# A hybrid residual block on one core: four seven-product pairs in the second feed-forward, a weight sum made by accumulating transfers, and four engines' issue order written out as a table

## The chip, the cores and the metric

The kernel runs on one core of a Trainium2 chip. The metric is the device time of one launch in microseconds (us). Engines: TensorE (PE in the rows), VectorE (DVE), ScalarE (ACT), GpSimd (POOL) and SyncE (SP, which issues most loads); transfers run on 16 DMA engines. Each engine takes its instructions in the order in which they were written to its queue and waits where an operand isn't ready.

## The reference

One layer of an encoder block on x of 256 tokens x 1024 channels, in float32:

```python
h = rmsnorm(x, ffn1_pre_g)
x = x + 0.5 * rmsnorm(swiglu(h, ffn1_w_in, ffn1_w_down), ffn1_post_g)
h = rmsnorm(x, mix_pre_g)              # gated recurrence, forgetting attention, merge
...
x = x + rmsnorm(y @ w_out, mix_post_g)
x = x + rmsnorm(mem_cross_attention(...), mem_post_g)
h = rmsnorm(x, ffn2_pre_g)
x = x + 0.5 * rmsnorm(swiglu(h, ffn2_w_in, ffn2_w_down), ffn2_post_g)

def swiglu(h, w_in, w_down):           # w_in 1024 x 5632, w_down 2816 x 1024
    gate, up = split(h @ w_in, 2)
    return (silu(gate) * up) @ w_down
```

The change concerns the second `swiglu`, and the order of everything.

## The kernel before

Every product is made of three: a float32 weight tile `raw` of 128x1024 is loaded (512 KB), ScalarE rounds it to `hi` and VectorE subtracts, `lo = raw - hi` (`load_split`, L151 to L155; `split`, L173 and L174, for tiles that are computed). PE then multiplies activation-hi by weight-hi, activation-hi by weight-lo and activation-lo by weight-hi, each a 128x512 matmul (`MM`, L100). There are 8 `hi` and 8 `lo` buffers, 4 `raw` ones and 4 of a tag "extra", whose tiles are called `sraw`.

A feed-forward (`ffn`, from L427) cuts its 2816 hidden columns into 11 chunks of 256 (512 columns of w_in, gate and up). A chunk is done directly (`act_tok`, `act_col`, `act_first`: 2 halves of the tokens x 8 blocks of channels x 3 = 48 matmuls, 4 weight tiles), or two chunks together as a pair (`act_pair`). A pair does the 2x2 block product (token halves by channel halves, and the weight's channel halves by the two chunks) with seven block products in place of eight, by sums of the blocks: 7 x 12 = 84 matmuls for two chunks. Its weight operands are, in order: `sums` (first loaded as one block, `of_x(0)`), then `sums + both`, then that plus block (1,1), block (1,1) itself, `both` plus block (1,1), block (1,0), and last the sum plus block (1,0). Each is two tiles, split to hi and lo (`splits`). The block sums are made either by VectorE (`add`, L596) or, for the pairs in the list FETCHED, by POOL with an accumulating load into the tile (`more`, L569, `both[j]` += block (1,1)). VectorE takes the four quarter results together (`c01` L645, `c11` L651, `c00` L661); `act_evac` does silu on ScalarE (L450) and the product with the up half on VectorE (L453, L455) to `at`; `flush` transposes `at` on PE (L445) to `tr` and splits it to `act`; `down` multiplies `act` by w_down into four accumulators. The downs of older chunks stand between a pair's products.

In the second feed-forward chunks 0, 1, 2, 5 and 8 are direct, and (3,4), (6,7) and (9,10) are pairs. Its tail is `post` (L416 to L421), which adds to `xs` and stores.

The order of each engine's queue is made by a scheduler from the order of the program, with hooks where it was corrected by hand: `tc.high_priority()`, `tc.issue_after(ins)`, and `after(i)`, which puts work behind the i-th matmul. At the start the weights come with the first layer's input in tiles `head`; ScalarE casts them (L828), makes `hlT` (L372) and `xf` (L832).

Of the kernel before, what the change touches and what calls it, by code (L numbers as in the profile page):

```python
# [18 lines left out]
P = 128  # L19
# [16 lines left out]
TOKS = {"f1_in": (3, 8), "f2_in": (2, 5, 8)}  # L36

PAIRS = {"f1_in": (4, 6, 9), "f2_in": (3, 6, 9)}
# [17 lines left out]
FETCHED = {"f1_in": (4, 6, 9), "f2_in": (3, 6, 9)}  # L56
# [11 lines left out]


# [16 lines left out]
def block_kernel(ctx: ExitStack, tc: tile.TileContext, wts, head_in, gf_in, x_in, mem_in, memT_in, cols, rows, fbias, masks, out):  # L86
    nc = tc.nc
    V, S, G, PE = nc.vector, nc.scalar, nc.gpsimd, nc.tensor

    cp = ctx.enter_context(tc.tile_pool(name="consts", bufs=1))  # L90
# [10 lines left out]

    @contextmanager
    def after(i):

        with tc.high_priority(), tc.issue_after(log[min(i, len(log) - 1)]):
            yield
# [37 lines left out]
    def load_split(src, n=512, behind=None, parts=None):  # L144

        raw = wp.tile([P, D], F32, tag="raw", name=nm("raw"), bufs=4)
        hi, lo = parts or parts_of()
        r, h, l = raw, hi, lo
        if n < 512:
            r, h, l = (p.rearrange("p (k n) -> p k n", k=2)[:, :, :n] for p in (raw, hi, lo))  # L150
        loads.append(nc.sync.dma_start(r, src).ins)  # L151
        with tc.issue_after(behind[0]) if behind else nullcontext():
            casts.append(S.copy(h, r).ins)  # L153
        with tc.issue_after(behind[1]) if behind else nullcontext():
            los.append(V.tensor_tensor(out=l, in0=r, in1=h.bitcast(F32), op=ALU.subtract).ins)  # L155
        return hi, lo
# [138 lines left out]
    def table(ins):  # L295

        with tc.issue_after(ins):
            S.activation(warm, ones[:, 0:1], AF.Abs_reciprocal_sqrt)
# [128 lines left out]
    def ffn(w_in, w_dn, X, r2, n_tok, i_row, first_half, second_half=None):  # L427
# [8 lines left out]
        def flush(n):  # L436

            if late:
                c = late.pop(0)
                tr = trp()  # L440
                trv = tr.rearrange("p (j t) -> p j t", j=2)
                with after(n):
                    for h in range(2):
                        for j in range(2):
                            PE.transpose(trv[:, j, h * P : (h + 1) * P], ats[c, h][:, j * P : (j + 1) * P], ident)  # L445
                    split(acts[c][:, 0], acts[c][:, 1], trv)
# [87 lines left out]
        def pair_inputs():  # L534
            for k in range(2):
              with tc.issue_after(evs[-1][1]):
                V.tensor_tensor(out=xf[k][:, :, P:], in0=xf[k][:, :, P:], in1=bc(row[:, :P], [P, 4, P], 1), op=ALU.mult)
# [33 lines left out]
        def act_pair(c, between):  # L571
# [55 lines left out]
            with tc.issue_after(last_silu[0]) if c - 2 in pairs else nullcontext():  # L627
                u = splits(sums)
# [5 lines left out]
            u = splits(sums)  # L634
            if "e" not in sx:
# [7 lines left out]
            with tc.high_priority():  # L643
                t = half_tile("c01")
                V.tensor_tensor(out=t, in0=b4, in1=v, op=ALU.subtract)  # L645
                act_evac(t, c, 0)
            product(b1, of("ad"), splits(both), False)
            S.copy(w, b1)
            with tc.high_priority():
                t = half_tile("c11")  # L650
                V.tensor_tensor(out=t, in0=p5, in1=w, op=ALU.subtract)  # L651
                act_evac(t, c, 1, r2[0], q)
# [5 lines left out]
            add(sums, raw)  # L658
            with tc.high_priority():
                t = half_tile("c00")  # L660
                V.tensor_tensor(out=t, in0=p1, in1=b0, op=ALU.add)  # L661
                act_evac(t, c + 1, 0)
# [7 lines left out]
            with tc.high_priority():  # L670
                silu = act_evac(b1, c + 1, 1, r2[0], q)
# [8 lines left out]
        def pair_loads(c):  # L680
            if c in pairs and c not in sums_of_pair:
                with tc.issue_after(loads[-1]):
                    sums_of_pair[c] = sum_load(c, 0, ((0, 0), (0, 1))), sum_load(c, 1, ((0, 1), (1, 1)))
# [17 lines left out]
        if callable(r2):  # L701
# [4 lines left out]
            for c in range(2):  # L706
                acts[c] = m4([P, 2, 2, T], F32R, "act")
                for h in range(2):
                    with tc.issue_after(casts[-1]):
                        silu = act_evac(outs[c][h], c, h)  # L710
# [3 lines left out]
        for c in range(n_tok, NFF):  # L714
# [42 lines left out]
            if c <= 6 <= last:  # L757
                grow = load_row(i_row)
                if first_half:
                    with tc.issue_after(loads[-1]):  # L760
                        nc.sync.dma_start(masks_s, masks)
# [58 lines left out]
    for kb in range(KB):  # L820
# [3 lines left out]
        for c in range(2):  # L824
            hi, lo = (p[:, kb % 2 * 512 : kb % 2 * 512 + 512] for p in cache[_AT["f1_in"] + 4 * c + kb // 2])
            w = heads[kb][:, HX : HX + 512] if c == 0 else raw1[kb // 2][:, kb % 2 * 512 : kb % 2 * 512 + 512]
            with tc.issue_after(lo_last):
                S.copy(hi, w)  # L828
# [5 lines left out]
    def norm_1():  # L834
        with tc.issue_after(loads[X_AT]):
            for h in range(2):
                nc.sync.dma_start(xs[:, h], x_in[:, h])
        with tc.issue_after(loads[-1]):
            nc.sync.dma_start(cols_s, cols)
            nc.sync.dma_start(fb_s, fbias)  # L840
# [7 lines left out]
    def half(X, r, h, g, *ms, into=None, act=True):  # L848

        for i, m in enumerate(ms):  # L850
            with after(m):
                to_T(X, x_blocks(h), h, g, (i,) if len(ms) == 2 else (0, 1), mm if X is X3 and h else trp)
# [30 lines left out]
    with tc.issue_after(iv_last):  # L883
        S.activation(le, le, AF.Exp)
# [220 lines left out]
    def forget(m):  # L1105
        pf = trp()
        with after(m):
            for h in range(2):
                PE.transpose(pf[0:8, h * P : (h + 1) * P], zf[h], ident)
        V.tensor_scalar(out=fz, in0=pf[0:8, :T], scalar1=fb_s, scalar2=None, op0=ALU.add)  # L1110
        V.scalar_tensor_tensor(out=fa, in0=fz, scalar=-1.0, in1=fz, op0=ALU.mult, op1=ALU.max)
        with tc.issue_after(sig_last):
            logs.append(S.activation(fa, fa, AF.Exp, scale=-1.0).ins)
# [37 lines left out]
    with after(r0):  # L1151
        for r in recs:
            r.grow(0)
    for si, ms in enumerate(SETS):
        with after(r0 + R_AT[si]):
            banks = [acc()]
            banks.append(acc() if ms[-1] in (1, 128) else banks[0])
            for j, m in enumerate(ms):
                for r in recs:
                    r.products(m, banks[r.g if m == 128 else j], j == 1)  # L1160
            with tc.issue_after(gf_last[1, 1]) if si == 1 else tc.issue_after(lo_at["k_b", 1]) if ms[-1] == 64 else nullcontext():
                for r in recs:
                    if ms[-1] < 128:
                        r.grow(ms[-1])
            with tc.issue_after(logs[1]) if ms[-1] == 32 else nullcontext():
                for m in ms:
                    for r in recs:
                        r.keep(m, LEVELS.index(m) if m < 64 else None)
        if si == FG:
            with tc.high_priority(), tc.issue_after(recs[1].grown):  # L1170
                forget_sums()
        if si < 2:
            with tc.high_priority(), tc.issue_after(gf_last[R_GROW[si]]):
                for r in recs:
                    r.grow(SETS[si + 1][0])
# [4 lines left out]
    for g in range(2):  # L1180
        kp = [wp.tile([P, D], F32R, tag="extra", name=nm("kp"), bufs=4).rearrange("p (i t) -> p i t", i=4) for _ in range(2)]
        qp = m4([P, 2, 4, P], F32R, n="qp")
        with tc.high_priority():
            for j in range(2):
                i2 = slice(2 * j, 2 * j + 2)
                with tc.issue_after(recs[1].last) if (g, j) == (0, 1) else nullcontext():
                    split(kp[0][:, i2], kp[1][:, i2], kb_[g][:, i2])
            for j in range(2):
                i2 = slice(2 * j, 2 * j + 2)
                split(qp[:, 0, i2], qp[:, 1, i2], qb_[g][:, i2, P:])  # L1190
# [67 lines left out]
    def fox_pT(g, m):  # L1258
        pT0 = m4([P, 4, T], n="pT0")
        pT1 = wp.tile([P, D], F32, tag="extra", name=nm("pT1"), bufs=4)[:, :512].rearrange("p (i s) -> p i s", i=4)  # L1260
        for h, b in ((0, 0), (1, 0), (1, 1)):
            tr = trp()
            with after(m + 5 * b):
                for i in range(4):
                    PE.transpose(tr[:, i * P : (i + 1) * P], ps_[g, h][:, i, b * P : (b + 1) * P], ident)
                trv = tr.rearrange("p (i s) -> p i s", i=4)
                if b == 0:
# [545 lines left out]
```

## Time and profile before

| | us |
|---|---|
| median of 3 runs | 767.94 (767.77 to 768.22) |
| the profiled execution | 767.82 |
| its span in the profile | 765.6 |
| from the second feed-forward's begin to the end of the span | 575 to 765.6 |
| the stretch from its chunk 5 on to the last lo | 629.4 to 742.4 |

The span goes from the first to the last instruction that the profile shows; 2.2 us of the execution lie outside of it. The clock granted to PE was 0.998 of full. "PE" in a row is the matmul, "PEld" its weight load. A row `L155 DVE TENSOR_TENSOR lo<-raw,hi ... x38 | 45.7, 1220 | 3.2 <-ACT hi L153 3.1` means: 38 instructions of line 155 on VectorE, 45.7 us busy, 1220 ns each, and 3.2 us idle ahead of them, of which 3.1 waiting for line 153 on ScalarE. Two instructions of an engine can overlap by some 0.1 us, so the time from one start to the next is what a row of them costs.

### The profile page before, as it was taken

The page shows a single profiled execution, that of the slowest core. Times are in us where ns is not written, and L with a number is a line of the kernel's source. Part 1 is how long each engine was busy: PE and PEld are TensorE (multiplying, and loading weights), DVE is VectorE, ACT ScalarE, POOL GpSimd, SP SyncE. Part 2 cuts the span into 40 slices and gives each one's busy share as a digit, 9 for nine tenths or more (in the row PEclk, how much of TensorE's full clock was granted, in tenths as well). Part 3 has the DMA queues.
Part 4 walks back from the last instruction along what each step waited for, and adds up shares of the span by engine and source line. Part 5 has one row for each costly group of instructions (what it writes and reads, how often), then busy time and mean ns, then how long its engine had stood idle before and what let it go on. Part 6 is the DMA issues. An engine that isn't in the chain of part 4 may idle for free.

```text
span 765.6 us, 11756 instructions
## 1 busy us (share of the span) xinstructions
PE 756.7 (99%) x4302; PEld 642.8 (84%) x4302; DVE 664.4 (87%) x982; ACT 521.2 (68%) x841; POOL 33.0 (4%) x56
## 2 busy tenths in 40 slices
PE   9999999999999999999999999999999999999996
PEld 8888888888888998898888888888887888888885
DVE  6799998988678898888689899999979899997973
ACT  8667576688774659667666755875968566675762
POOL 0000000000000100200001000001000100000000
PEclk9999999999999999999999999999999999999999
DMA  9778777674745545835668955586386837868641
GB/s 350 235 259 245 214 239 275 182 252 167 233 158 149 185 137 183 284 128 182 189 220 245 267 183 186 175 286 131 114 291 191 257 108 257 236 222 269 176 131 55
DMA packets 47146, 157.88 MB, mean 206 GB/s; under 512 B 5385, under 2 KB 9105, under 8 KB 47089
## 3 DMA queue, kind: packets, MB, share of 16 engines
q1 hardware_dynamic: 43168, 144.83, 55.5%
q0 software_dynamic: 3488, 11.94, 8.7%
q8 instruction: 33, 0.54, 0.3%
q10 hardware_dynamic: 432, 0.37, 0.2%
q14 instruction: 25, 0.20, 0.1%
HBM read 156.06 MB, written 1.06 MB: 205 GB/s over the span
## 4 chain that ended last, share of the span: by engine, by line
PE 85%; DVE 8%; ACT 2%; DMA 2%; issue 1%; DVEq 0%; ACTq 0%
PE mm L100 45%; PE acc L100 33%; PE tr L100 5%; DVE lo L155 2%; DMA raw<-in_wts_dram 2%; PE tr L445 1%; DVE lo L174 1%; ACT hi L153 1%; PE tr L385 1%; DVE xs L421 1%; DVE sraw L1393 1%; DMA head<-in_head_dram 0%; DVE post L416 0%; DVE sx L174 0%; DVE qm L1578 0%
## 5 line engine op out<-in xcount | busy, mean ns | idle before, releaser
L155 DVE TENSOR_TENSOR lo<-raw,hi 128x1024 fp32r<-128x1024 f32 (+1 forms) x188 | 222.3, 1199 | 29.5 <-ACT hi L153 26.2
L153 ACT CAST hi<-raw 128x1024 fp32r<-128x1024 f32 (+1 forms) x188 | 190.9, 1033 | 50.3 <-DMA raw<-in_wts_dram 29.7
L100 PE MATMUL mm<-hi,hlT 128*128 128x512 f32 (+1 forms) x632 | 191.6, 382 | 0.0
L100 PEld LDWEIGHTS mm<-hi,hlT 128*128 128x128 f32 x632 | 116.7, 188 | 20.2
L100 PE MATMUL mm<-lo,hlT 128*128 128x512 f32 (+1 forms) x316 | 119.1, 381 | 0.0
L100 PE MATMUL acc<-hi,act 128*128 128x512 f32 x352 | 113.6, 390 | 0.0
L173 ACT CAST hi<-sraw 128x1024 fp32r<-128x1024 f32 x80 | 83.3, 1052 | 33.9 <-DVE sraw L596 15.6
L174 DVE TENSOR_TENSOR lo<-sraw,hi 128x1024 fp32r<-128x1024 f32 x80 | 96.1, 1221 | 3.8 <-ACT hi L173 3.4
L100 PE MATMUL mm<-hi,sx 128*128 128x512 f32 x280 | 90.8, 391 | 0.0
L100 PEld LDWEIGHTS acc<-hi,act 128*128 128x128 f32 x352 | 66.2, 188 | 13.4
L100 PE MATMUL acc<-lo,act 128*128 128x512 f32 x176 | 69.5, 395 | 0.0
L100 PEld LDWEIGHTS mm<-lo,hlT 128*128 128x128 f32 x316 | 59.3, 188 | 10.0
L100 PEld LDWEIGHTS mm<-hi,sx 128*128 128x128 f32 x280 | 52.5, 188 | 10.9
L100 PE MATMUL acc<-hlT,hi 128*128 128x512 f32 x240 | 60.7, 394 | 0.0
L100 PE MATMUL mm<-lo,sx 128*128 128x512 f32 x140 | 54.9, 392 | 0.0
L100 PEld LDWEIGHTS acc<-hlT,hi 128*128 128x128 f32 x240 | 43.1, 189 | 7.7 <-DVE hlT L373 0.2
L174 DVE TENSOR_TENSOR lo<-raw,hi 128x1024 fp32r<-128x1024 f32 x32 | 38.6, 1221 | 2.1 <-ACT hi L173 2.0
L173 ACT CAST hi<-raw 128x1024 fp32r<-128x1024 f32 x32 | 33.1, 1053 | 8.5 <-issue 3.1
L100 PEld LDWEIGHTS acc<-lo,act 128*128 128x128 f32 x176 | 33.1, 188 | 6.4
L100 PE MATMUL acc<-lo,hT 128*128 128x512 f32 x96 | 37.8, 393 | 0.0
L100 PE MATMUL acc<-hi,hT 128*128 128x512 f32 x96 | 37.7, 392 | 0.1
L100 PE MATMUL acc<-hi,lT 128*128 128x512 f32 x96 | 37.3, 391 | 0.0
(329 smaller groups left out, 1232.4 us busy)
## 6 DMA issues: line engine op xcount, KB each, us to landing
raw<-in_wts_dram SPq DMA_DIRECT2D x215, 512.0 KB, 4.6
sraw<-in_wts_dram SPq DMA_DIRECT2D x32, 512.0 KB, 6.6
sraw<-in_wts_dram POOLq DMA_DIRECT2D x20, 512.0 KB, 5.9
raw<-in_gf_dram SPq DMA_DIRECT2D x12, 344.0 KB, 3.7
head<-in_head_dram SPq DMA_DIRECT2D x7, 392.0 KB, 6.4
grow<-in_rows_dram SPq DMA_DIRECT2D x4, 512.0 KB, 7.6
xs<-in_x_dram SPq DMA_DIRECT2D x2, 512.0 KB, 7.6
cb<-cd POOLq DMA_DIRECT2D x2, 512.0 KB, 4.9
```

The lines of the kernel that those rows point to most:

```text
L100: log.append(PE.matmul(*args, **kw).ins)
L153: casts.append(S.copy(h, r).ins)
L155: los.append(V.tensor_tensor(out=l, in0=r, in1=h.bitcast(F32), op=ALU.subtract).ins)
L173: a = S.copy(hi, src)
L174: b = V.tensor_tensor(out=lo, in0=src, in1=hi.bitcast(F32), op=ALU.subtract)
L385: PE.transpose(blocks[-1][1], src(kb), ident)
L421: summed = V.scalar_tensor_tensor(out=xh, in0=ts[a // 512][:, a % 512 : (b - 1) % 512 + 1], scalar=r, in1=xh, op0=ALU.mult, op1=ALU.add)
L445: PE.transpose(trv[:, j, h * P : (h + 1) * P], ats[c, h][:, j * P : (j + 1) * P], ident)
L1393: V.tensor_tensor(out=x, in0=x, in1=y, op=ALU.add)
```

## The change

1. In the second feed-forward TOKS becomes (2,) and PAIRS (3, 5, 7, 9): chunks 5 and 8 are no longer direct, and 3 to 10 are four pairs in a row. FETCHED names all four.
2. A new list FETCHED_LAST (those four pairs): the last product's weight sum is made by two accumulating loads of block (1,0) on POOL's queue, issued behind the third split, in place of two additions on VectorE. Block (1,0) is still loaded on its own for the product before.
3. All hooks are taken out. `issue()`, called at the end, reads a table ISSUE with the complete order of PE's, VectorE's, ScalarE's and SP's instructions, as runs "first+count" of the program's own numbering, and chains each instruction to the one before it. POOL's order is not in the table.

```diff
-TOKS = {"f1_in": (3, 8), "f2_in": (2, 5, 8)}
-
-PAIRS = {"f1_in": (4, 6, 9), "f2_in": (3, 6, 9)}
+TOKS = {"f1_in": (3, 8), "f2_in": (2,)}
+
+PAIRS = {"f1_in": (4, 6, 9), "f2_in": (3, 5, 7, 9)}
...
-FETCHED = {"f1_in": (4, 6, 9), "f2_in": (3, 6, 9)}
+FETCHED = {"f1_in": (4, 6, 9), "f2_in": (3, 5, 7, 9)}
+FETCHED_LAST = {"f1_in": (), "f2_in": (3, 5, 7, 9)}
...
+ISSUE = {
+    "PE": (
+        "0+124 154+2 124+6 156 130+10 157+2 140+6 159+2 146+8 161+25 190+14 186 204+20 187+3 224+28 286+3 252+34 290+8 289 298+73 386 371+14 387+2 385 390+6 "
...
+    def issue():
+        traced = [i for i in nc.cur_bb.bb.instructions if i.opcode != "TilePoolBoundary"]
+        for name, runs in ISSUE.items():
+            own = [i for i in traced if i.engine == getattr(mybir.EngineType, name)]
+            order = []
+            for run in runs.split():
+                first, _, n = run.partition("+")
+                order += own[int(first) : int(first) + int(n or 1)]
+            assert len(order) == len(own), (name, len(order), len(own))
+            for before, ins in zip(order, order[1:]):
+                tc.add_manual_dep(ins, before.name, mybir.DependencyInfo(mybir.DependencyClass.NoSync, mybir.DependencyReason.DATA))
...
-                with after(n):
-                    for h in range(2):
-                        for j in range(2):
-                            PE.transpose(trv[:, j, h * P : (h + 1) * P], ats[c, h][:, j * P : (j + 1) * P], ident)
-                    split(acts[c][:, 0], acts[c][:, 1], trv)
+                for h in range(2):
+                    for j in range(2):
+                        PE.transpose(trv[:, j, h * P : (h + 1) * P], ats[c, h][:, j * P : (j + 1) * P], ident)
+                split(acts[c][:, 0], acts[c][:, 1], trv)
...
-            with tc.issue_after(last_silu[0]) if c - 2 in pairs else nullcontext():
-                u = splits(sums)
+            u = splits(sums)
...
             raw = raws(1, 1)
             add(sums, raw)
             u = splits(sums)
+            if c in FETCHED_LAST[w_in]:
+                for j in range(2):
+                    more(sums[j], c, 1, 0, j, ALU.add)
...
-            add(sums, raw)
-            with tc.high_priority():
-                t = half_tile("c00")
-                V.tensor_tensor(out=t, in0=p1, in1=b0, op=ALU.add)
-                act_evac(t, c + 1, 0)
+            if c not in FETCHED_LAST[w_in]:
+                add(sums, raw)
+            t = half_tile("c00")
+            V.tensor_tensor(out=t, in0=p1, in1=b0, op=ALU.add)
+            act_evac(t, c + 1, 0)
```

The instructions by engine, before and after: PE 3966 and 3954 (12 matmuls of 128x512 fewer; 210 transposes in both, in 48 runs before and 110 after, of which 64 are of one), VectorE 984 and 991, ScalarE 782 and 793 (one of them a table load more), POOL 61 and 71, SP 292 in both, in another order.

What the table and the pairs do to the queues is seen at four places. In the rows a name ends in two numbers, of the name and of the buffer's tile; line numbers of the changed kernel are higher (L248 is the `split` subtraction, L667 `add`, L640 the accumulating load, L182 `MM`, L517 `flush`, L894 the head's cast).

VectorE, third weight operand of the second pair in the chain. Before, in pair (6,7):

```order
L453 TENSOR_TENSOR at_1454_6941<-mm_1452_6914,sg_1453_6939 128x256
L596 TENSOR_TENSOR sraw_1455_6943<-sraw_1455_6943,raw_1480_7046 128x1024
L596 TENSOR_TENSOR sraw_1456_6945<-sraw_1456_6945,raw_1481_7047 128x1024
L174 TENSOR_TENSOR lo_1483_7053<-sraw_1455_6943,hi_1482_7052 128x1024
L174 TENSOR_TENSOR lo_1485_7057<-sraw_1456_6945,hi_1484_7056 128x1024
```

Now, in pair (5,6):

```order
L667 TENSOR_TENSOR sraw_1435_6853<-sraw_1435_6853,raw_1460_6956 128x1024
L248 TENSOR_TENSOR act_1363_6536<-tr_1432_6842,act_1363_6536 128x512
L248 TENSOR_TENSOR lo_1459_6928<-sraw_1436_6855,hi_1458_6927 128x1024
L248 TENSOR_TENSOR lo_1463_6963<-sraw_1435_6853,hi_1462_6962 128x1024
L667 TENSOR_TENSOR sraw_1436_6855<-sraw_1436_6855,raw_1461_6957 128x1024
L248 TENSOR_TENSOR lo_1465_6967<-sraw_1436_6855,hi_1464_6966 128x1024
```

The second addition moved behind the first tile's lo, so that the second tile's lo, whose hi ScalarE casts from the added tile, follows it at once. The same stands in pair (7,8).

POOL, the accumulating loads of the second feed-forward. Before:

```order
L569 DMA sraw_1361_6532<-in_wts_dram 128x1024
L569 DMA sraw_1362_6534<-in_wts_dram 128x1024
L569 DMA sraw_1457_6947<-in_wts_dram 128x1024
L569 DMA sraw_1458_6949<-in_wts_dram 128x1024
L569 DMA sraw_1552_7358<-in_wts_dram 128x1024
L569 DMA sraw_1553_7360<-in_wts_dram 128x1024
```

Now, the first three of the four pairs (of each the two `both` tiles, then the two `sums` tiles):

```order
L640 DMA sraw_1361_6532<-in_wts_dram 128x1024
L640 DMA sraw_1362_6534<-in_wts_dram 128x1024
L640 DMA sraw_1359_6528<-in_wts_dram 128x1024
L640 DMA sraw_1360_6530<-in_wts_dram 128x1024
L640 DMA sraw_1437_6857<-in_wts_dram 128x1024
L640 DMA sraw_1438_6859<-in_wts_dram 128x1024
L640 DMA sraw_1435_6853<-in_wts_dram 128x1024
L640 DMA sraw_1436_6855<-in_wts_dram 128x1024
L640 DMA sraw_1506_7142<-in_wts_dram 128x1024
L640 DMA sraw_1507_7144<-in_wts_dram 128x1024
L640 DMA sraw_1504_7138<-in_wts_dram 128x1024
L640 DMA sraw_1505_7140<-in_wts_dram 128x1024
```

Each pair has four where it had two, and one more pair has them.

PE, a flush beside a pair's products. Before:

```order
L100 MATMUL acc_1350_6507<-hi_1520_7208,act_1435_6853 128x512
L445 MATMUL tr_1526_7239<-ident_74,at_1498_7121 128x128 x2
L445 MATMUL tr_1526_7239<-ident_74,at_1505_7148 128x128 x2
L100 MATMUL acc_1350_6507<-lo_1521_7209,act_1435_6853 128x512
L100 MATMUL acc_1350_6507<-hi_1520_7208,act_1435_6853 128x512
```

Now:

```order
L182 MATMUL tr_1486_7074<-lo_1490_7080,hlT_1225_5960 128x512
L517 MATMUL tr_1500_7125<-ident_74,at_1478_7033 128x128
L182 MATMUL tr_1486_7074<-hi_1489_7079,hlT_1225_5960 128x512
L517 MATMUL tr_1500_7125<-ident_74,at_1478_7033 128x128
L182 MATMUL tr_1486_7074<-hi_1489_7079,hlT_1225_5960 128x512
```

Four transposes in a row became single ones between the matmuls of a product.

ScalarE, the head. Before:

```order
L814 ACTIVATE warm_1_79<-ones_72 128x1
L832 ACTIVATE xf_6_91<-head_8_93 128x256
L828 CAST hi_21_131<-head_8_93 128x512
L828 CAST hi_23_133<-raw_9_96 128x512
L828 CAST hi_21_131<-head_10_98 128x512
L372 ACTIVATE hlT_2_87<-head_10_98 128x256
L828 CAST hi_23_133<-raw_9_96 128x512
L832 ACTIVATE xf_6_91<-head_10_98 128x256
L828 CAST hi_25_149<-head_11_101 128x512
```

Now:

```order
L894 CAST hi_21_131<-head_8_93 128x512
L894 CAST hi_23_133<-raw_9_96 128x512
L445 ACTIVATE hlT_2_87<-head_10_98 128x256
L898 ACTIVATE xf_6_91<-head_8_93 128x256
L894 CAST hi_21_131<-head_10_98 128x512
L894 CAST hi_23_133<-raw_9_96 128x512
L445 ACTIVATE hlT_3_88<-head_11_101 128x256
L881 ACT_TABLE_LOAD
L881 ACTIVATE warm_1_79<-ones_72 128x1
L894 CAST hi_25_149<-head_11_101 128x512
```

The casts moved ahead of `xf`, and a table load (with the `warm` activation) moved to a place between `hlT` and the third head's cast.

197 lines of the change are left out of this document (80 added, 117 removed), and 58 rows, old and new, of the table ISSUE.

## The prediction

> **What bounds the kernel now.** I read the page first: engine shares, the slices, the chain of work that ended last.
>
> ```profile
> span 765.6 us, 11756 instructions
> PE 756.7 (99%) x4302; PEld 642.8 (84%) x4302; DVE 664.4 (87%) x982; ACT 521.2 (68%) x841; POOL 33.0 (4%) x56
> ...
> DVE  6799998988678898888689899999979899997973
> ...
> DMA  9778777674745545835668955586386837868641
> ...
> PE 85%; DVE 8%; ACT 2%; DMA 2%; issue 1%; DVEq 0%; ACTq 0%
> ```
>
> TensorE (PE) is busy 99% of the span and is 85% of the chain. A busy PE is no proof that every slot is used, so next come the chain in order of time (start, length, what) and PE's waits (total, times, longest).
>
> ```profile
> 629.51 2.72 PE mm L100 x12
> 632.23 2.72 PE acc L100 x12
> ...
> 739.93 19.09 PE acc L100 x84
> ```
> ```profile
> PE tr L100 <- PEq L1802: 0.8, 1, 0.8
> PE tr L385 <- DVE xs L421: 0.7, 1, 0.7
> PE tr L445 <- DVE at L455: 0.3, 1, 0.3
> PE acc L1662 <- DVE sm L1652: 0.2, 1, 0.2
> PE acc L100 <- ACT hi L828: 0.2, 1, 0.2
> ```
>
> Twelve 128x512 matmuls back to back take 2.72 us, 0.2267 us each; the "busy" mean of such a matmul on the page is a pipelined length, not its price. The five longest waits are 2.2 us together: little is left to win except by doing less on PE. That puts all weight on whoever feeds PE in the stage that changes. The windows view gives that stage (the pairs of the second FFN), and a stretch of the first FFN in which two pairs follow each other directly:
>
> ```profile
> core 0: us, PE busy (x) PEld busy (x) DVE busy (x) ACT busy (x) POOL busy (x), PEclk, DMA share, GB/s
> 629.40:742.40 113.00, 112.68 (x513) 93.08 (x512) 104.47 (x112) 78.83 (x99) 3.38 (x4) 1.00 0.69 219
> 67.00:97.00 30.00, 30.00 (x138) 24.79 (x137) 29.79 (x33) 21.39 (x28) 1.69 (x2) 1.00 0.78 238
> 645.00:655.00 10.00, 10.00 (x48) 8.29 (x47) 8.47 (x11) 6.51 (x10) 0.00 (x0) 1.00 1.01 374
> ```
>
> In 113.0 us PE lacks 0.3 us, VectorE (DVE) is idle 8.5 us, the DMA engines are busy 0.69. The third row shows plain loads at the full rate: 374 GB/s, so one 512 KB load is 1.4 us of all 16 engines.
>
> **The change, part by part.** *Matmuls.* Chunks 5 and 8 were computed directly, 48 matmuls each; now chunks 5 to 8 are two pairs of 84 (7 products of 12), where before there were one pair and two direct chunks: 84 + 96 = 180 against 168. Twelve matmuls at 0.2267 us: **-2.72 us** on PE, all on the path.
>
> *VectorE.* The rows by line (busy total, mean ns), and two rows of its timeline:
>
> ```profile
> L174 DVE TENSOR_TENSOR lo<-sraw,hi 128x1024 fp32r<-128x1024 f32 x30 | 36.1, 1223 | 2.5 <-ACT hi L173 2.4
> L596 DVE TENSOR_TENSOR sraw<-sraw,raw 128x1024 f32<-128x1024 f32 x12 | 14.5, 1223 | 1.4 <-DMA raw<-in_wts_dram 1.3
> L645 DVE TENSOR_TENSOR c<-mm,vw 128x512 f32<-128x512 f32 x3 | 2.1, 689 | 0.0
> ```
> ```profile
> 723.93 1.22 DVE L174 TENSOR_TENSOR lo<-raw,hi 128x1024 fp32r<-128x1024 f32 x1
> 725.06 1.22 DVE L174 TENSOR_TENSOR lo<-sraw,hi 128x1024 fp32r<-128x1024 f32 x1
> ```
>
> From start to start a 128x1024 operation costs 1.13 us; a 128x512 one by the same overlap (0.09) 0.60. In the built orders VectorE has six lo subtractions more (28 weight tiles in two pairs, against 14 in one pair and 8 in two direct chunks), two sum additions fewer and three c-halves more: 6 x 1.13 - 2 x 1.13 + 3 x 0.60 = +6.3 us. PE gives back 2.7 us of time in the same stage, so VectorE's idle shrinks by 9.0 us, and it had 8.5. It still has its lead at the stage's end: the last lo began at 741.13 and PE first read it at 746.15:
>
> ```profile
> 741.13 1.23 DVE L155 TENSOR_TENSOR lo<-raw,hi 128x1024 fp32r<-128x1024 f32 x1 [0.56 <-ACT hi L153]
> ```
> ```profile
> 746.15 0.39 PE L100 MATMUL acc<-lo,act 128*128 128x512 f32 x1
> ```
>
> 746.15 - 742.36 = 3.8 us ahead. So 8.5 + 3.8 - 9.0 = **3.3 us** is all that VectorE may newly wait before PE stalls at the end. That consecutive pairs can run so is shown by 67 to 97 us: DVE 29.79 of 30, PE 30.00 of 30, no stall. The order shows new waits. In pairs 5 and 7 a lo stands right behind the sum's second addition, and between them ScalarE has to cast; the cast's row is
>
> ```profile
> L173 ACT CAST hi<-sraw 128x1024 fp32r<-128x1024 f32 x30 | 31.2, 1053 | 8.9 <-PE mm L100 4.1 <-DVE sraw L596 4.0 <-ACT hi L173 0.8
> ```
>
> 1.05 us and a handoff, say 1.2 us at two places: 2.4 us of the 3.3. Behind it on VectorE are queued the other lo's, for which PE waits. With them come the waits on loads (below). I take +0.5 us of new stall on PE, between 0 (the 3.3 us hold) and +7 (rival D). ScalarE's six casts and four copies more, about 6 x 1.05 + 4 x 0.6, lie in its idle 34 us of that window; they cost nothing unless they arrive late, which is the same wait.
>
> *Transfers.* Ten accumulating loads are added (6 to 16), on POOL's queue, and take the place of two additions per pair (the sum of the last product now, of three pairs). The DMA part for 629.4 to 742.4 us (packets, MB, share) and the issues (median to landing):
>
> ```profile
> q1 hardware_dynamic: 6192, 22.55, 58.3%
> q0 software_dynamic: 576, 2.10, 10.6%
> ...
> raw<-in_wts_dram SPq DMA_DIRECT2D x34, 512.0 KB, 4.5
> sraw<-in_wts_dram SPq DMA_DIRECT2D x8, 512.0 KB, 7.3
> ```
>
> Four accumulating loads take 10.6% of 113 us: 3.0 us each, twice a plain one (58.3% over 43 transfers: 1.5 us). A pair with two down chunks now has 12 plain and 4 accumulating loads: 12 x 1.4 to 1.5 + 4 x 3.0 = 29 to 30 us, in a PE period of 132 x 0.2267 + 8 transposes x 0.11 = 30.8 us: the DMA engines are 94 to 99% taken in three consecutive pairs. They have never been shown to be so for 90 us; they were for 10 (row above, 1.01), with PE unstalled. A load issued while two accumulate lands after 7.3 us (median of sraw, SP) rather than 4.5. This is the largest unknown; my +0.5 us contains it in the sense that three us of lead hold it.
>
> In a sentence beside it: the Trainium skill ("Trainium Kernel Development and Optimization", section Key Constraints) says that loads issued from SP, ACT and POOL run on the same 16 DMA engines and interleave; the trace agrees (7.3 against 4.5 us), so that the POOL queue is no extra bandwidth.
>
> *Transposes.* PE's order now puts most of the 210 transposes one by one between matmuls, where they stood in runs of 4 (see the order rows). The timeline has runs of 2, 4 and 8:
>
> ```profile
> 158.19 0.38 PE L445 MATMUL tr<-ident,at 128*128 128x128 f32 x2
> ...
> 158.64 0.40 PE L100 MATMUL mm<-hi,sx 128*128 128x512 f32 x1
> ```
> ```profile
> 622.97 0.60 PE L445 MATMUL tr<-ident,at 128*128 128x128 f32 x4
> ...
> 623.63 0.40 PE L100 MATMUL acc<-hi,act 128*128 128x512 f32 x1
> ```
> ```profile
> 589.14 1.03 PE L385 MATMUL tr<-ident,xs 128*128 128x128 f32 x8
> ...
> 590.24 0.63 PE L100 MATMUL mm<-hi,hlT 128*128 128x512 f32 x2
> ```
>
> From the run's start to the second matmul behind it: 0.45, 0.66, 1.10 us. Less one matmul slot (0.227) that is 0.22, 0.43, 0.87: 0.11 us a transpose and no fixed part. A run of one isn't in the trace; by this line it costs 0.11 like the others, and splitting costs **0**. (The ends: 0.06, a quarter slot, if its weight load hid, rival B; 0.12 if a run has a small fixed part, 62 more runs x 0.01 = +0.6.)
>
> *The head.* ScalarE's order there has a second table load, between hlT and the cast of head 2's weights; its row's price and the old order:
>
> ```profile
> 1.18 1.28 ACT L814 ACT_TABLE_LOAD   x1 [1.18 <-PEq L1802]
> 4.17 0.51 ACT L832 ACTIVATE xf<-head 128x256 f32<-128x256 f32 x1 [1.50 <-DMA head<-in_head_dram]
> ...
> 8.40 0.61 ACT L828 CAST hi<-head 128x512 fp32r<-128x512 f32 x1
> ```
>
> The cast that began at 8.40 feeds PE's 25th matmul, at 5.24 + 24 x 0.2267 = 10.7 us (5.24 is PE's first). Queued behind hi, xf, hlT and a 1.28 + 0.2 us load it would end at about 10.9: 0.2 us late. The first cast now comes ahead of xf, 0.4 us sooner, of which the next head's arrival takes most back. I take **+0.2 us** (0 to +0.8, as the x and column loads were moved up among the head loads too).
>
> *The rest of the table.* Outside the second FFN PE's matmuls are the same; the order changes who is waited for. Of PE's waits above, the 0.7 at xs goes down by about 0.1 (its post now stands ahead of a lo, 0.6 us sooner, but PE also arrives two matmuls sooner); 0.3 at L455 belongs to the old end. I take **-0.6 us**, between -2.2 (all five go) and +1.5 (as many new ones as VectorE's order brings; it's 90% full or more in most slices).
>
> **The sum.** -2.72 + 0.5 + 0 + 0.2 - 0.6 = -2.6 us, against the profiled execution's own 767.82 us (span 765.6 and 2.2 around it; the median of the runs is 767.94, so 0.1 more): **765.2 us**.
>
> **Rivals.** *B, more than the matmuls goes.* Either all five waits go (-2.2 in place of -0.6: 763.6) or single transposes get cheaper. If a lone transpose's weight load ran under the 512-column matmul ahead, each new run would save some 0.11 - 0.06 = 0.05 us, 62 times (48 runs before, 110 after): -3.3 us, 765.2 - 3.3 = 761.9. I take 762.5 for the two together. Against it: in the three rows above the first transpose of a run, which has such a matmul ahead, is no cheaper than the others. 0.22. Beside it: the Trainium skill's page "TensorE: Matmul & The Clock Gate" (section "LDWEIGHTS (loading the stationary operand)", and its words on the reorder window) lets PE pull a weight load ahead of a running matmul, and puts a 128-column load at P/1.2, 107 ns. The measured 110 ns look like that load unhidden; by its rule of pulling ahead the time would be B's, 761.9.
>
> *C, nothing measurable.* VectorE's waits use the 3.3 us and 1.5 to 4 us more, PE stalls eat the matmuls: 766.4 to 769.4, say 767.5. For it: 2.4 us of the 3.3 are gone by the two casts alone. 0.24.
>
> *D, the other side: the accumulating loads fill the DMA engines.* In pairs 5, 7 and 9 the sums wait for loads that land in 7 to 9 us instead of 4.5; VectorE stands behind the first addition, and with it all lo's. Price: 3 us a pair, three pairs, 9 us less the 3.3 in hand, +5.7 on PE: 767.8 - 2.7 + 5.7 = 771. It decides (slower than 769.5) once VectorE loses over 3.3 + 2.7 + 1.5 = 7.5 us, 2.5 us a pair. For it: 94 to 99% DMA use. Against it: loads may be issued early where buffers are free, and 10 us at 1.01 cost PE nothing. 0.20.
>
> **How the numbers follow.** Forecast (764 to 766.4) 0.34, B 0.22, C 0.24, D 0.20. About 0.2%, 1.5 us, is what a measurement of this kernel tells from no change: faster is 0.34 + 0.22 = 0.56, the same 0.24, slower 0.20. The range takes in most of B, all of C and D's beginning: 761.5 to 770.0; the forecast's own is 764.0 to 766.4.
>
> **What would show it.** Matmuls of 128x512 down by 12, spacing still 0.2267 us; in the second FFN's pairs DVE over 97% busy with PE's share unchanged; q0's share there about three times as high. Wrong, if a lone transpose takes 0.06 us from its neighbours' starts (B), if PE's waits name lo or sraw for over 4 us together (C, D), or sraw from POOL lands after 9 us and VectorE's waits name it (D).

## The result and the profile after

| kernel | median us | runs | ratio to before |
|---|---|---|---|
| before | 767.36 (766.65 to 768.22) | 6 | 1 |
| changed | 775.38 (771.85 to 777.75) | 6 | 1.0097, 95% 1.0079 to 1.0115 |

The change makes the kernel 1% slower, 8 us, and its runs spread over 6 us where those of before spread over 1.6. The profiled execution took 777.75 us (span 776.0), the longest of the six, so what its rows give is 2.4 us more than the median has. The page:

```profile
span 776.0 us, 11798 instructions
PE 758.7 (98%) x4290; PEld 638.9 (82%) x4290; DVE 667.5 (86%) x989; ACT 526.7 (68%) x852; POOL 40.2 (5%) x66
...
PE 80%; DMA 8%; DVE 8%; ACT 2%; issue 2%; SPq 0%; DVEq 0%; ACTq 0%
```

PE has 12 instructions fewer, and is 80% of the chain in place of 85%; DMA went from 2% to 8%. PE was busy 2.0 us longer all the same (758.7 against 756.7), in part because it ran on at half its clock for 3.4 us after one of its waits (last section). PE's waits, where before had 2.2 us in five:

```profile
PE tr L458 <- DVE xs L494: 2.4, 1, 2.4
PE tr L517 <- DVE at L525: 2.2, 2, 1.3
PE tr L182 <- DVE q_b L301: 1.5, 1, 1.5
PE acc L182 <- ACT hi L894: 0.9, 2, 0.5
PE mm L182 <- DVE zg L1368: 0.8, 1, 0.8
PE tr L517 <- DVE at L527: 0.8, 1, 0.8
...
PE acc L182 <- DVE lo L229: 0.7, 2, 0.6
```

These are 9.3 us; with the 0.8 us at the start that before has too, and one wait of 0.4, they are 10.5 against 2.2. Where they lie, by windows (length; PE, PEld, DVE, ACT and POOL busy; PEclk, DMA share, GB/s):

```profile
20.00:40.00 20.00, 18.70 (x86) 15.12 (x86) 14.91 (x38) 14.11 (x25) 1.30 (x2) 1.00 0.70 218
320.00:345.00 25.00, 23.45 (x159) 21.33 (x158) 19.59 (x43) 14.94 (x30) 2.57 (x2) 1.00 0.39 127
575.00:595.00 20.00, 17.64 (x75) 14.25 (x75) 13.16 (x29) 12.96 (x32) 0.00 (x0) 0.91 0.50 182
630.00:724.00 94.00, 94.00 (x426) 77.10 (x425) 87.19 (x94) 65.35 (x82) 9.32 (x11) 1.00 0.88 258
724.00:742.40 18.40, 16.64 (x75) 13.20 (x74) 18.40 (x21) 15.27 (x21) 2.56 (x3) 1.00 0.91 210
```

PE loses 1.3, 1.6, 0.8 (at `zg`, 372 us) and 2.4 us in four places ahead of the second feed-forward's pairs, and 0.0 of 94 us in most of the pairs, the stretch that I had feared most. In the last pair it loses 1.8 us, with VectorE busy all of the time. What a place looks like, at 37 us (ScalarE, VectorE, PE):

```profile
36.77 1.05 ACT L228 CAST hi<-raw 128x1024 fp32r<-128x1024 f32 x1 [3.78 <-DMA raw<-in_wts_dram]
37.73 0.46 ACT L522 ACTIVATE sg<-acc,facs 128x256 f32<-128x256 f32 x1
```
```profile
37.86 1.22 DVE L229 TENSOR_TENSOR lo<-raw,hi 128x1024 fp32r<-128x1024 f32 x1 [3.65 <-ACT hi L228]
39.00 0.41 DVE L525 TENSOR_TENSOR at<-acc,sg 128x256 f32<-128x256 f32 x1
```
```profile
39.47 0.33 PE L517 MATMUL tr<-ident,at 128*128 128x128 f32 x1 [1.30 <-DVE at L525]
```

The silu `sg` stands in ScalarE's queue behind a cast that waits 3.8 us for its load; `at` stands on VectorE behind that tile's lo; PE's transpose waits for `at`. That cast is the sixth of a 128x1024 tile. In the kernel before the sixth waits for its load too, 1.4 us, but ScalarE has done the four silus and the cast of `act` ahead of it:

```profile
26.51 1.55 ACT L450 ACTIVATE sg<-acc,facs 128x256 f32<-128x256 f32 x4
...
33.26 0.59 ACT L173 CAST act<-tr 128x512 fp32r<-128x512 f32 x1 [2.60 <-PE tr L445]
35.27 1.05 ACT L153 CAST hi<-raw 128x1024 fp32r<-128x1024 f32 x1 [1.42 <-DMA raw<-in_wts_dram]
```

At 330 us a ScalarE copy (`plo`) stands in the same way behind a cast that waits 3.76 us for its load, and `q_b`, for which PE waits, on VectorE behind a tile's lo; in the kernel before no cast waits for a load between 318 and 331 us.

### The profile page after: what moved, and what is told of

Read it like the earlier page. It is cut to its first block, busy times and chain, and to the rows that moved or that the text cites. A ratio compares the mean times of both kernels' runs of the same rounds, so it can differ in the third digit from the quotient of the medians.

```text
span 776.0 us, 11798 instructions
## 1 busy us (share of the span) xinstructions
PE 758.7 (98%) x4290; PEld 638.9 (82%) x4290; DVE 667.5 (86%) x989; ACT 526.7 (68%) x852; POOL 40.2 (5%) x66
## 4 chain that ended last, share of the span: by engine, by line
PE 80%; DMA 8%; DVE 8%; ACT 2%; issue 2%; SPq 0%; DVEq 0%; ACTq 0%
PE mm L182 39%; PE acc L182 34%; DMA raw<-in_wts_dram 6%; PE tr L182 4%; DVE lo L248 3%; DVE lo L229 2%; ACT hi L228 1%; DMA grow<-in_rows_dram 1%; PE tr L458 1%; DVE sraw L667 1%; DMA head<-in_head_dram 1%; PE tr L517 1%; DMA sraw<-in_wts_dram 1%; PE tr L1316 0%; DVE act L248 0%
## 5 line engine op out<-in xcount | busy, mean ns | idle before, releaser
L229 DVE TENSOR_TENSOR lo<-raw,hi 128x1024 fp32r<-128x1024 f32 (+1 forms) x180 | 212.3, 1195 | 30.5 <-ACT hi L228 27.4
L228 ACT CAST hi<-raw 128x1024 fp32r<-128x1024 f32 (+1 forms) x180 | 182.8, 1030 | 51.7 <-DMA raw<-in_wts_dram 32.4
L182 PE MATMUL mm<-hi,hlT 128*128 128x512 f32 (+1 forms) x576 | 176.7, 384 | 0.8 <-DVE zg L1368 0.8
L247 ACT CAST hi<-sraw 128x1024 fp32r<-128x1024 f32 x90 | 92.9, 1051 | 44.5 <-DVE sraw L667 31.8
L182 PEld LDWEIGHTS mm<-hi,hlT 128*128 128x128 f32 x576 | 105.6, 188 | 19.4 <-DVE zg L1368 1.3
L182 PE MATMUL acc<-hi,act 128*128 128x512 f32 x352 | 115.0, 394 | 0.0
L248 DVE TENSOR_TENSOR lo<-sraw,hi 128x1024 fp32r<-128x1024 f32 x90 | 108.0, 1217 | 4.8 <-ACT hi L247 4.5
L182 PE MATMUL mm<-lo,hlT 128*128 128x512 f32 (+1 forms) x288 | 109.1, 383 | 0.0
L182 PE MATMUL mm<-hi,sx 128*128 128x512 f32 x320 | 104.4, 393 | 0.0
L182 PEld LDWEIGHTS acc<-hi,act 128*128 128x128 f32 x352 | 65.7, 188 | 14.1
L182 PE MATMUL acc<-lo,act 128*128 128x512 f32 x176 | 69.3, 394 | 0.7 <-DVE lo L229 0.7
L182 PEld LDWEIGHTS mm<-hi,sx 128*128 128x128 f32 x320 | 59.6, 188 | 12.4
L182 PE MATMUL mm<-lo,sx 128*128 128x512 f32 x160 | 62.8, 392 | 0.0
L182 PEld LDWEIGHTS mm<-lo,hlT 128*128 128x128 f32 x288 | 54.1, 188 | 9.1
L182 PE MATMUL acc<-hlT,hi 128*128 128x512 f32 x240 | 60.3, 393 | 0.0
L182 PEld LDWEIGHTS acc<-hlT,hi 128*128 128x128 f32 x240 | 43.2, 189 | 7.7
L248 DVE TENSOR_TENSOR lo<-raw,hi 128x1024 fp32r<-128x1024 f32 x36 | 43.2, 1217 | 2.8 <-ACT hi L247 2.8
L182 PEld LDWEIGHTS acc<-lo,act 128*128 128x128 f32 x176 | 33.1, 188 | 8.1 <-DVE lo L229 1.6
L182 PE MATMUL acc<-hi,hT 128*128 128x512 f32 x96 | 38.2, 397 | 0.0
L182 PE MATMUL acc<-lo,hT 128*128 128x512 f32 x96 | 38.1, 397 | 0.0
L182 PE MATMUL acc<-hi,lT 128*128 128x512 f32 x96 | 37.9, 396 | 0.0
```

Of the source, the lines that this page charges most:

```text
L182: log.append(PE.matmul(*args, **kw).ins)
L247: a = S.copy(hi, src)
L248: b = V.tensor_tensor(out=lo, in0=src, in1=hi.bitcast(F32), op=ALU.subtract)
```

## The experiments

Theory 1: the loss is new waits that the table's order brings, ready work queued behind work that waits for a load, most of it outside the pairs. Theory 2 is the prediction's rival D (accumulating loads fill the transfers), theory 3 that single transposes cost more. Ratios are to the kernel before, measured beside each run (its medians 767.1 to 767.5 us).

| run | us | ratio, 95% |
|---|---|---|
| e1 old order to 600 us | 767.73 | 0.9997 (0.9983 to 1.0011) |
| e2 grow earlier | 776.38 | 1.0121 (1.0100 to 1.0142) |
| e3 pairs and last sum, no table | 776.29 | 1.0119 (1.0099 to 1.0139) |
| e4 pairs, no last sum, no table | 776.52 | 1.0113 (1.0088 to 1.0139) |
| e5 c00 ahead | 768.06 | 1.0005 (0.9996 to 1.0014) |
| e6 old order to 100 us | 772.74 | 1.0067 (1.0044 to 1.0091) |
| e7 old order to 345 us | 769.71 | 1.0027 (1.0012 to 1.0043) |
| e8 no third sum in the last pair | 766.37 | 0.9984 (0.9973 to 0.9995) |
| e9 no accumulating loads | 766.26 | 0.9982 (0.9968 to 0.9995) |
| e10 third sum on GpSimd | 770.22 | 1.0040 (1.0027 to 1.0054) |
| e11 silu ahead of cast | 772.61 | 1.0064 (1.0050 to 1.0077) |
| e12 last sum only | 767.53 | 1.0000 (0.9991 to 1.0008) |
| e13 table's order ahead, old pairs | 779.07 | 1.0149 (1.0135 to 1.0164) |
| e14 neither third sum nor accumulating | 764.78 | 0.9966 (0.9954 to 0.9978) |
| e15 copies ahead | 767.04 | 0.9998 (0.9988 to 1.0008) |

### The order ahead of the pairs

**e1.** In the table of the changed kernel, per engine:

```diff
-    (the table's order of all instructions)
+    (before's order of what began before 600 us there, then the table's order of the rest)
```

> The changed kernel, with its table rewritten for the first part: up to what began before 600 us (all ahead of the first pair of the second feed-forward) the four engines have the order of the kernel before; from there on the table's order. Theory 1 (the loss is new waits that the table's order brings outside the pairs): PE's new idle up to 590 us goes, by the changed kernel's gaps 0.7 + 0.5 in the head, 1.5 at 37.9, 0.3 at 172, 1.7 at 328.6, 1.0 at 371 and 3.4 more than before at 581 to 588, about 9 us: 766 to 767 us. Theory 2 (the accumulating loads saturate the transfers, rival D): they are all still there, the time stays over 772. Theory 3 (transposes one by one cost PE more than in runs): two thirds of them are back in runs of 4, a part of the loss goes evenly, 771 to 773, and the named gaps stay.

767.73 us: 7.7 of the 8 us are gone. The gaps at 37.9, 328 and 371 are gone, at xs too; one place in the last pair is left (below), and two new waits of 0.3 and 0.4 us at 94 and 160 us. Neither theory 2 nor theory 3 allowed that. The order put back is that of all four engines, SP's loads too.

**e6 and e7**, the same with the cut at 100 and at 345 us.

> The changed kernel with the old order up to 100 us alone (head and the first direct chunks). Theory 1, each place pays for itself: the gaps of the head (0.7 and 0.5) and at 37.9 (1.5 us) go, 772.5 to 773.5. Rival (a late place earlier gives the loads time, and takes away a wait later): within 1 us of the changed kernel.

> The changed kernel with the old order up to 345 us. Theory 1: the gaps at 172 (0.3) and 328.6 (1.7) go as well, 770.5 to 771.5; what is left to 767.7 are the gaps at 371 and at 581. Rival: as with 100 us, later waits take their place, 773 to 776.

772.74 and 769.71: about 2.6, 3.0 and 2.0 us for the three stretches, each uncertain by some 2 us by the intervals of the ratios, where PE's gaps in them say 2.7, 2.0 and 4.4. Each stretch costs something by itself; how much, these runs tell only roughly.

**e13**, the other way round: before's three pairs and order, behind the table's order.

> The other way round: the kernel before with its three pairs and its own order from the first pair on (608 us in the changed kernel's trace), and ahead of that the table's order. No new pair, no added accumulating load. If the table's order ahead of the second feed-forward costs by itself what the runs up to 100, 345 and 600 us summed to (7.7 us): 774 to 776. If it costs only together with the new pairs: 767 to 769.

779.07, over what was expected. The two orders don't fit where they were joined, 616 to 642 us, as PE's waits show:

```profile
PE tr L513 <- DVE at L521: 2.8, 2, 1.9
PE mm L178 <- ACT sx L243: 2.5, 1, 2.5
```

The second row and 0.9 of the first lie at the joint; from 600 to 645 us PE was idle for 4.0 us in all. The other 7 to 8 us are the table's order, without any new pair.

**e2**, one load of the changed kernel moved in SP's table:

```diff
 raw_1246  raw_1249  raw_1252  raw_1282  raw_1283  raw_1284  raw_1287  grow_1218
-(grow behind six weight loads)
+(grow between raw_1246 and raw_1249, as in the kernel before)
```

> The changed kernel, with one load moved in SP's table: the row 'grow' of the memory branch's post is issued ahead of the last six weight loads, where the kernel before has it, in place of behind them. Theory 1: PE's wait at xs (2.4 us, and 4.3 us of gaps at 581 to 588, where before had 0.8) goes to about 1, the time falls by 3 us, to 772 to 773. Theories 2 and 3: no change, within 1 us of 775.

A miss: 776.38. In the changed kernel grow was late, 7.8 us from its issue, and VectorE's post waited for it:

```profile
573.49 7.79 DMA grow<-in_rows_dram
```
```profile
581.30 0.69 DVE L489 SCALAR_TENSOR_TENSOR post<-acc,grow 128x512 f32<-128x512 f32 x1 [2.87 <-DMA grow<-in_rows_dram]
```

With grow moved that wait is gone, and PE waits a few matmuls sooner for another:

```profile
572.91 0.50 PE L182 MATMUL acc<-lo,hT 128*128 128x512 f32 x1 [0.28 <-DVE lo L229]
574.93 0.63 PE L182 MATMUL acc<-hi,lT 128*128 128x512 f32 x1 [1.53 <-DVE lT L248]
575.36 0.63 PE L182 MATMUL acc<-hi,hT 128*128 128x512 f32 x1
```

`lT` stands on VectorE behind lo's whose loads were now behind grow (a cast waits 3.83 us for one of them). What I took for one late load was a stretch in which several loads are late against this order; moving one moved the wait.

**e11**, the place at 37 us:

```diff
-ScalarE: CAST hi_109 ; ACTIVATE sg_85      VectorE: lo_110 ; at_86
+ScalarE: ACTIVATE sg_85 ; CAST hi_109      VectorE: at_86 ; lo_110
```

> The changed kernel (775.4), with two neighbours exchanged in the table at 37 us: ScalarE does chunk 1's last silu ahead of the cast that waits 3.8 us for its load, and VectorE the product 'at' ahead of that tile's lo. If the order itself (work that is ready, queued behind work that waits for a load) is the cause: PE's gap of 1.5 us ahead of the transpose at 37.9 goes, with nothing in its place, 773.5 to 774.5. If the loads are what is late and any order would wait for them: PE waits as long for the lo behind it, 775 to 776.

772.61, 2.8 us less than the changed kernel and more than expected, but not as expected: the gap at 37.9 went, and 2 us later PE waited for the next thing behind the same cast, `act`:

```profile
PE acc L182 <- DVE act L248: 1.1, 1, 1.1
```
```profile
37.26 1.05 ACT L228 CAST hi<-raw 128x1024 fp32r<-128x1024 f32 x1 [4.08 <-DMA raw<-in_wts_dram]
38.22 0.58 ACT L247 CAST act<-tr 128x512 fp32r<-128x512 f32 x1
```

So the exchange itself gained some 0.2 us (a wait of 1.3 became one of 1.1): I had moved the silu alone, and the cast of `act`, which the kernel before has ahead of that cast too (33.26 against 35.27 above), stayed behind it. The rest came from other places. At xs PE waited 1.1 in place of 2.4 us, and its clock stayed at full behind that (1.00 from 575 to 600 us, where the changed kernel's profile has 0.93). Why grow came sooner there I can't show.

One thing is open. That the order ahead of the pairs costs 7.7 us is shown from both sides (e1, e13). Which part of it lies in the place of ready work on ScalarE and VectorE, and which in the order of SP's loads, is not: e1, e6, e7 and e13 change both, e11 only the first at half of one place, e2 only the second, for one load.

### The pairs

**e3 and e4**, the change without its table:

```diff
 # kernel before, hooks and scheduler kept
-TOKS (2, 5, 8)  PAIRS, FETCHED (3, 6, 9)
+TOKS (2,)       PAIRS, FETCHED (3, 5, 7, 9)     # e3: FETCHED_LAST too; e4: not
```

> The kernel before with its hooks and the scheduler's order, and of the change only the lists: four pairs, all fetched, and the last sum by accumulating loads (10 more of them, 12 matmuls fewer). No table. Theory 1: the 2.7 us of the matmuls come through but for what VectorE lacks: 764.7 to 767.5, faster than before. Theory 2: the transfers are as full as in the changed kernel, over 770.

> As the run with four pairs under the scheduler's order, but the last sum is added by VectorE (8 additions of 1.13 us more, 8 accumulating loads of 3.0 us fewer). Theory 1: VectorE has 15 us more to do than before in a stage with 8.5 idle, 3.8 us of lead and 2.7 us less time, so PE stalls by 6 us: 768 to 772, slower than the run with accumulating loads. Theory 2: the transfers have room again, faster than that run.

Both numbers of theory 1 were missed, e3's by 9 us and e4's by 4.5, and accumulating or adding made no difference (776.29 and 776.52). In both PE stands in the pairs, here 630 to 742.4 us of e3 and of e4:

```profile
630.00:742.40 112.40, 105.33 (x462) 84.56 (x461) 98.96 (x105) 75.15 (x96) 10.19 (x12) 0.98 0.85 248
```
```profile
630.00:742.40 112.40, 102.91 (x458) 82.77 (x457) 108.78 (x116) 76.13 (x97) 5.06 (x6) 1.00 0.67 210
```

The first row is e3, the second e4. In e4 VectorE is 97% busy, the lack that was worked out. In e3 it is 88%, with transfers at 0.85, and PE still lacks 7 us, most of it waiting for `at` (4.9 us). Its hooks were written for three pairs, which may be why; no run tests that. e1 and e3 have the same work, and up to 600 us nearly PE's waits of before; behind it one has the table's order and one the scheduler's, 767.73 against 776.29: from 600 us on the table is worth 8.6 us. Ahead of that it loses about as much.

**What eats the matmuls' 2.7 us in e1.** VectorE in the last pair, and PE:

```profile
714.40 1.22 DVE L659 TENSOR_TENSOR sraw<-sraw,sraw 128x1024 f32<-128x1024 f32 x1 [0.46 <-DMA sraw<-in_wts_dram]
715.54 0.68 DVE L724 TENSOR_TENSOR c<-vw,tr 128x512 f32<-128x512 f32 x1
...
717.27 0.42 DVE L517 TENSOR_TENSOR at<-c,sg 128x256 f32<-128x256 f32 x1
```
```profile
PE tr L509 <- DVE at L517: 1.8, 1, 1.8
PE tr L509 <- DVE at L519: 1.6, 3, 0.8
```

The first row and 0.8 of the second lie here, 2.6 us of idle time; from start to start of the matmuls it is 3.0. c00's product was done at 711.4; c00 ran at 715.5, behind two additions. **e5** moves it:

```diff
-VectorE: lo at(c01) add at(c11) add c00 lo at(c00) add lo at(e) add lo
+VectorE: lo at(c01) at(c11) c00 add at(c00) add at(e) lo lo add add lo
-ScalarE: cast sg(c00) cast sg(e)
+ScalarE: sg(c00) cast sg(e) cast
```

> The kernel with the old order up to 600 us and the table's from there (767.7), with one place of the table changed: in the last pair VectorE does c00 and the two products 'at' behind it ahead of the additions and lo's that they stand behind in the table, and ScalarE their silu ahead of the casts. Theory 1a (the pairs' 2.7 us are eaten by PE's two waits of 2.0 and 1.0 us for 'at', since c00 is queued behind a sum's addition that waits for its load): the waits fall from 3.0 to under 1 us, the time to 765 to 766, faster than before by 0.2 to 0.3%. Rival 1b (VectorE has no time there: the moved work only delays the lo's behind it, and PE waits for those): 767 to 768, PE's waits at lo in place of those at 'at'.

768.06, rival 1b: the waits at `at` are all but gone, and others stand there, 1.5 us with a second copy of 0.3. The idle time is 1.1 us shorter, but no gain shows in the times (768.06 and 767.73, intervals that overlap):

```profile
PE mm L174 <- DVE lo L240: 0.7, 1, 0.7
PE mm L174 <- ACT vw L680: 0.4, 1, 0.4
```

**e8, e9, e14** then leave out of the computation VectorE's two additions of the last pair's third weight sum (e8, on e5), all 16 accumulating loads of the second feed-forward (e9, on e1), and both (e14, on e5). They show what this work costs, and don't compute the block:

```diff
-            add(sums, raw)
+            if (w_in, c) != ("f2_in", 9):     # e8, e14
+                add(sums, raw)
...
-            if c in FETCHED[w_in]:
+            if c in FETCHED[w_in] and w_in != "f2_in":     # e9, e14
...
-            if c in FETCHED_LAST[w_in]:
+            if False:                                      # e9, e14
```

> The kernel with c00 ahead (768.1), without the two additions of the last pair's third weight sum (left out of the computation: 2.26 us less on VectorE, the transfers unchanged). If VectorE's time is what the pairs lack there: PE's waits of 2.0 us at lo and act in that pair go, 765.5 to 766.3. If it is the transfers (rival D): the waits stay, 767.5 to 768.5.

> The kernel with the old order up to 600 us and the table's from there (767.7), without the 16 accumulating loads of the second feed-forward (left out of the computation: 16 x 3.0 = 48 us less for the 16 transfer engines, VectorE's work unchanged). If VectorE's place and time set the pairs' waits: PE still waits for 'at' in the last pair, 767 to 768, since c00 stands behind the addition whose load is alone late. If the full transfers make the loads late (rival D): the wait of 3.0 us goes, 764.5 to 765.5.

> The kernel with c00 ahead (768.1), without the last pair's two third-sum additions and without the second feed-forward's 16 accumulating loads (both left out of the computation). If VectorE's time and the late loads together eat the matmuls' gain: 764.7 to 765.5, the full 2.7 us below 767.5, with no PE wait over 0.5 us in the pairs. If something else does (the copies on ScalarE, which free the PSUM banks): 766 to 767, as with either alone, and PE waits for vw.

766.37, 766.26 and 764.78. Each alone gives 1.5 to 1.7 us (e8 about what VectorE's side expected, e9 between the two sides, its interval overlapping e1's), and with each PE still waits (e8 for a copy, e9 for `at`):

```profile
PE mm L174 <- ACT vw L704: 1.6, 1, 1.6
```
```profile
PE tr L509 <- DVE at L519: 1.2, 2, 0.8
PE tr L509 <- DVE at L517: 1.0, 1, 1.0
```

Both together give 3.3 us and, within the interval, the full gain. The stretch 629.4 to 742.4 in e9 and in e14:

```profile
629.40:742.40 113.00, 111.15 (x503) 90.64 (x503) 105.50 (x114) 80.07 (x102) 0.00 (x0) 1.00 0.56 194
```
```profile
629.40:742.40 113.00, 113.00 (x514) 92.62 (x513) 105.72 (x115) 82.38 (x104) 0.00 (x0) 1.00 0.57 198
```

So what eats the gain in the last pair is VectorE's time and the time of the accumulating loads together. Equal parts are what the medians say; the loads' part is the less certain, and no run shows how they cost it. **e10 and e15** look for that time with the whole computation done:

```diff
-            add(sums, raw)                                             # VectorE
+            add(sums, raw, G if (w_in, c) == ("f2_in", 9) else V)      # e10, on e5
```
```diff
-ScalarE: cast act vw act cast                  VectorE: lo act lo
+ScalarE: act vw cast cast act                  VectorE: lo lo act     # e15, on e5
```

> The kernel with c00 ahead (768.1), with the last pair's two additions of the third weight sum done by GpSimd in place of VectorE; everything is computed. If VectorE's time is the lack and GpSimd adds a 128x1024 tile within some 3 us: 765.5 to 766.5, faster than before. If GpSimd is slower than that, or slows VectorE by its own accesses: PE waits for the third operand, 768 to 772.

> The kernel with c00 ahead (768.1), and in the last pair also ScalarE's copy of the first product (vw) ahead of the two casts it stands behind, and VectorE's lo of the third operand's second tile ahead of an act. Everything is computed. If the copies' place is what costs: PE's waits for vw and lo (0.6 + 0.9 us) go, 766.3 to 767. If VectorE is late anyway: no change, 767.5 to 768.5.

e10 is slower than e5 by 2.2 us (770.22): GpSimd takes 5.56 us for the two additions, where VectorE takes 2.3:

```profile
718.31 5.56 POOL L659 TENSOR_TENSOR sraw<-sraw,raw 128x1024 f32<-128x1024 f32 x2 [0.45 <-DVE lo L240]
```

The copies are worth 0.5 to 1 us at most (ratio 0.9998 against 1.0005, intervals that overlap); no version with the whole computation beats the kernel before.

**e12**, the kernel before with FETCHED_LAST for its three pairs:

> The kernel before (three pairs, hooks, the scheduler's order), with the last weight sum of its three pairs by accumulating loads: 6 more of them, 6 additions fewer on VectorE. If accumulating loads are harmless where VectorE isn't short: 766.7 to 768, no change. If they make the other loads late (rival D): 769 or more.

767.53: six accumulating loads more, six additions fewer, no change. In the kernel before, where PE waits for neither, the exchange is free.

## Why the prediction was wrong

- **The rest of the table: the step that failed.** It stood at -0.6 us, between -2.2 and +1.5. The order ahead of 600 us measured +7.7 (775.38 against e1's 767.73), of which the head, a term of its own, is some 0.7. I bounded the term by the waits that PE had before, as if the new order could only take from those or add as many again. The order showed more: at 37 us silus behind casts, each cast behind a load. I looked for that in the second feed-forward alone. Forecast and range (to 770.0) fell with it, and so did the direction.
- **Matmuls, -2.72:** right; with the cover in place e14 is 2.4 us below the kernel before (ratio 0.9966, 0.9954 to 0.9978).
- **VectorE, +0.5 with 3.3 us in hand:** mis-sized. Rival C had the right mechanism and price, in the last pair: e1 loses 3.0 us there, as much as the matmuls gave. The changed kernel shows how (window 630 to 726): VectorE waited for casts, and these waited for VectorE's sums more than for loads, the handoff that the prediction counted at two places.

```profile
DVE lo L248 <- ACT hi L247: 5.4, 7, 1.2
ACT hi L247 <- DVE sraw L667: 13.9, 7, 2.5
ACT hi L247 <- DMA raw<-in_wts_dram: 4.1, 4, 1.6
```

  VectorE was 93% busy up to 724 us, not over 97, and PE lost nothing; behind that it had no time left (18.40 of 18.40 us), and PE lost 1.8.
- **Transfers, rival D:** not what made the kernel slower. The estimate of 94 to 99% (its own terms give 94 to 97) measured 0.88, with PE at 94.00 of 94.00; their part is the 1.5 us of e9, by the medians. The price of 3.0 us held, 14 accumulating loads in 37.9% of 113 us. The 7.3 us to landing of `sraw` was read as the accumulating loads' doing; with 14 of them in place of 4 it is 5.3 (629.4 to 742.4 us):

```profile
q0 software_dynamic: 2016, 7.34, 37.9%
sraw<-in_wts_dram SPq DMA_DIRECT2D x12, 512.0 KB, 5.3
```

- **Transposes, 0:** right, and rival B fell (its product, 62 x 0.05, is 3.1 and not 3.3 us). A run of one in the changed kernel:

```profile
723.63 0.27 PE L517 MATMUL tr<-ident,at 128*128 128x128 f32 x1
723.66 0.47 PE L182 MATMUL mm<-lo,hlT 128*128 128x512 f32 x1
723.97 0.62 PE L182 MATMUL mm<-hi,hlT 128*128 128x512 f32 x2
```

  From the run's start to the second matmul behind it 0.34 us, one slot and 0.11, on the line of 0.45, 0.66 and 1.10 for 2, 4 and 8.
- **The head, +0.2 (0 to +0.8):** 0.9 us of waits at hi (two, 0.5 the longest) where before had 0.2: +0.7, inside its bounds but far from the value taken.
- **Not priced at all:** PE's clock after a wait, below; 1.7 us in the profiled execution.

## What to carry to other kernels

A complete issue order can lose where loads arrive later than it counts on. In each queue, look for work that is ready standing behind work that waits for a load, follow who waits for it, and price every such place, not those beside the edit alone. An engine's spare time has to be counted up to the last use, with the waits that come before it; and a wait that ends at one late load can be a stretch of late loads, so that moving the one moves the wait, as e2 did. Splitting transposes among matmuls was free here, and so was trading additions for accumulating loads in the kernel before (e12).

## What the runs showed of the hardware that I had not expected

**PE's clock halves after some waits.** After the wait at xs PE ran on at 0.43 us a matmul for some 3.4 us; e13 did so behind a wait of 1.9 us at 37 us (length, PE busy, ..., PEclk):

```profile
584.50:588.20 3.70, 3.70 (x13) 3.07 (x13) 2.99 (x6) 2.79 (x9) 0.00 (x0) 0.54 0.32 124
```
```profile
40.20:43.40 3.20, 3.20 (x10) 2.49 (x9) 3.20 (x5) 1.89 (x4) 0.00 (x0) 0.52 0.91 328
```

Each such stretch costs another 1.5 to 1.7 us (0.48 of 3.20 us, 0.46 of 3.70), busy by the profile. The length of the wait does not decide it: e2's wait of 1.5 us, with one of 0.3 ahead of it, was followed by such a stretch (its rows above, 0.43 us from 574.93 to 575.36), while e1's of 1.8 us left the clock at 1.00, and so did one of 2.8 us in e3, in which PE was busy for 1.21 of 4.00 us:

```profile
652.00:656.00 4.00, 1.21 (x9) 0.76 (x8) 4.00 (x7) 1.72 (x2) 0.85 (x1) 1.00 1.00 176
656.00:660.00 4.00, 4.00 (x20) 3.31 (x19) 4.00 (x5) 1.94 (x3) 0.00 (x0) 1.00 1.00 329
```

The Trainium skill ("TensorE: Matmul & The Clock Gate", section "What's actually happening") has the clock at half after an idle window of about 3.4 us, in windows that run freely and don't start with the work. Half the clock and the length of the stretch agree with the rows. The idle window does not: waits of 1.5 to 2.4 us within a busy kernel were enough here. That the phase of such a window decided which waits were followed by it was not tested.
